# A hybrid attention and RWKV layer on one core: last group of the output projection by tiles, rotary rows double-buffered, small loads moved to the first phase

## Chip, core, metric

One Trainium2 chip, one of its cores. The metric is the device time of one execution in microseconds. TensorE (PE) multiplies matrices, VectorE (DVE), ScalarE (ACT) and GpSimd (POOL) compute element by element, and SyncE (SP) and ScalarE issue transfers (DMA).

## Reference

The layer takes 1024 prompt rows and 64 sample rows of width 1024, normalises them, sends them through one projection, and runs two groups of heads on its columns: differential attention (8 heads) and RWKV-7 (16 heads of 64). Cut to what matters here:

```python
h = _rms_norm(x, norm_pre, NORM_EPS)
proj = h @ w_in
q = _partial_rope(proj[..., A_Q:A_K].reshape(...), pos)      # the first 16 of 64 dims
k = _partial_rope(proj[..., A_K:A_V].reshape(...), pos)
lam = (jnp.exp(jnp.sum(lam_q1 * lam_k1)) - jnp.exp(jnp.sum(lam_q2 * lam_k2)) + lambda_init)
o = _diff_attend(q, k_all, v_all, pos, k_pos, lam)           # sample rows: cached k and v ahead
...
yb, s_T = _wkv_scan(rh, hs(decay), kh, vh, -kk, kk * ah, wkv0)
...
mix = jnp.concatenate([y_a, yb], axis=-1)                    # 2048 wide, both gated
out = mix @ w_out                                            # 2048 x 1024
x_new = x + _rms_norm(out, norm_post, NORM_EPS)
```

## The kernel before

All products are in fp32 precision: both operands are split into a rounded part and the rest (`wh`/`wl`, `hhi`/`hlo`, `mxh`/`mxl`), and three matmuls make one product. ScalarE makes the rounded part (a cast), POOL the rest (a subtraction; the helper's line is L158 for both the mix and the weights).

The work has four parts. The first normalises the rows and projects the first columns. `phase_b` runs the RWKV units, a chain of small steps on DVE, ScalarE and TensorE, while `filler()` projects the remaining columns as work for TensorE in between. `phase_a` runs attention head by head: `prep(h)` loads `qa`, `ka` (each in four transfers, from `rots` and `scr` in DRAM), the cached keys `ck`, and `vl`, `vn`, `ga`, and casts them to `qs` and `k`; scores `s`, exponentials `e`, transposed weights `wt` and outputs `x_o` follow. `out_projection` multiplies the mix with `w_out` and is woven with attention, except for its end.

Of the q and k columns the first 16 dims of each head are rotated. `proj` stores them in DRAM (`rots[kd, g, 0]` and, with the halves swapped, `rots[kd, g, 1]`; kd is q or k, g one of two sets of four heads), and `rope(kd, g)` handles them in 8 chunks of 136 columns: three loads on ScalarE's queue (`ra`, `rb`, `rt`, one buffer each for q and for k), three DVE operations (L965 to L967), and a store on SP's queue. The attention of head 0 needs `(q, 0)` and `(k, 0)`, that of head 4 `(q, 1)` and `(k, 1)`.

`out_projection` has groups (L1054): a range of k tiles of 128 rows and the column halves of 512. A job is a group and one of nine token tiles (the ninth has the 64 sample rows). `load_wo(g)` loads and splits a group's weights in pieces of 256 columns (`wor`, 4 buffers), `load_mix(q)` a job's mix. Groups 0 to 5 have four k and one half; 6 and 7 have two k and both halves. Each half's product comes in a PSUM tile (two of these) and is added to `part` by DVE (L1157). After its last group a tile is finished: sum of squares on ScalarE, two small steps on POOL (L1126, and the power -0.5 in L1127), then columns 0 to 767 on DVE (L1130, L1132) and the other 256 on ScalarE and POOL (L1129, L1131, L1133), where `npb` is the weight of the last norm and `fx` the input rows.

Two things set the order. `Weave` simulates costs and emits streams by rank (`yield` gives a stream's waiting time or condition); then a scheduler makes one list per engine, with tiles and their buffers. Each engine runs its list in order. Transfers go over eight lanes, and a transfer waits for the earlier one on its lane.

Of the kernel before, what the change touches and what calls it, by code (L numbers as in the profile page):

```python
# [1040 lines left out]
def out_projection(tc, I, O, E):  # L1041

    nc = tc.nc
    mm, act, stt, vtt, gtt, gts = (E[k] for k in ("mm", "act", "stt", "vtt", "gtt", "gts"))
# [72 lines left out]

    def finish(tt):
        o_ = part[tt]
        n = P if tt < 8 else TS  # L1120
        x_ = op.tile([P, D], F32, tag="x", bufs=2, name=f"fx{tt}")
        nc.scalar.dma_start(out=x_[:n], in_=x_rows(tt))
        sq = op.tile([P, D], BF16, tag="sq", name=f"fs{tt}")
        ms = op.tile([P, 1], F32, tag="ms", bufs=2, name=f"fm{tt}")
# [361 lines left out]
```

## Time and profile before

| | |
|---|---|
| three timed runs, median (lowest to highest) | 1856.12 us (1855.7 to 1856.61) |
| profiled execution: its own time | 1855.12 us |
| its span in the trace | 1853.3 us |
| busy in the span | PE 1691.8, DVE 1254.4, ACT 849.8, POOL 737.2 us |

The span is 1.8 us shorter than the time of the same execution; the rest lies around it. The windows below are in microseconds from the start of the span: RWKV with filler lies up to about 1246, attention begins after 1258, the output projection alone fills the end from about 1710. Row groups below carry line numbers of the kernel before.

### The profile page before, as it was taken

To read this page: it belongs to the slowest core of one execution; us is meant where nothing else is said; L and a number is where in the kernel's file an instruction comes from. 1 tells how busy PE (TensorE), PEld (TensorE's weight loads), DVE (VectorE), ACT (ScalarE), POOL (GpSimd) and SP (SyncE) were. 2 spreads that over 40 slices of the span, in tenths; PEclk is the share of its full clock that TensorE was granted. 3 is DMA by queue.
4 is the path that set the end of the run, shared out by engine and by line. 5 is a ranking of instruction groups with operands and counts; after the bars stand their busy time and mean duration, and the time that the engine had idled before them with its cause. 6 is when DMAs were issued, how large, how long until landed. Compare 5 with 4: busy or idle time off the path is not lost. (4 is left out here: it accounts for less than half of the span.)

```text
span 1853.3 us, 34474 instructions
## 1 busy us (share of the span) xinstructions
PE 1691.8 (91%) x12930; PEld 1505.7 (81%) x12930; DVE 1254.4 (68%) x2588; ACT 849.8 (46%) x2027; POOL 737.2 (40%) x938
## 2 busy tenths in 40 slices
PE   6999899899998999999999899997889888999995
PEld 5888888888888888888888789886879777787883
DVE  5568777777777787886876776524576655676236
ACT  5534444344344344434343434333556566576323
POOL 4442333233233333323332322113434456666757
PEclk8999999999999999999999899997999889999998
DMA  4110111231122110111101122345555655454425
GB/s 145 50 56 27 50 48 48 79 86 35 39 72 61 52 45 30 39 52 34 57 24 49 51 64 58 88 114 160 158 152 151 179 134 146 126 152 127 121 85 183
DMA packets 204240, 158.82 MB, mean 86 GB/s; under 512 B 44229, under 2 KB 185194, under 8 KB 204074
## 3 DMA queue, kind: packets, MB, share of 16 engines
q1 hardware_dynamic: 169242, 137.33, 25.8%
q10 hardware_dynamic: 34832, 19.30, 4.1%
q8 instruction: 102, 1.67, 0.4%
q14 instruction: 64, 0.52, 0.1%
HBM read 108.67 MB, written 47.34 MB: 84 GB/s over the span
## 5 line engine op out<-in xcount | busy, mean ns | idle before, releaser
L1146 PE MATMUL po<-woh,mxh 128*128 128x512 f32 x288 | 120.9, 420 | 7.4 <-DVE part L1157 5.9
L1147 PE MATMUL po<-woh,mxl 128*128 128x512 f32 x288 | 115.9, 402 | 2.4 <-POOL mxl L158 2.4
L1340 ACT ACTIVATE e<-s,nb 128x128 f32<-128x128 f32 (+7 forms) x144 | 101.0, 706 | 35.2 <-DVE nb L1333 19.7
L1148 PE MATMUL po<-wol,mxh 128*128 128x512 f32 x288 | 115.0, 400 | 1.9 <-POOL wol L158 1.9
L158 POOL TENSOR_TENSOR mxl<-mxr,mxh 128x512 fp32r<-128x512 f32 (+1 forms) x72 | 86.4, 1201 | 75.3 <-ACT mxh L157 66.7
L812 ACT ACTIVATE sd<-suv,dc 64x64 f32<-64x64 f32 x128 | 44.4, 347 | 152.9 <-DVE suv L843 148.7
L1323 PE MATMUL s<-k,qs 128*128 128x512 f32 (+4 forms) x208 | 80.0, 393 | 20.4 <-ACT k L1250 11.4
L1333 DVE TENSOR_REDUCE nb<-s 128x1 f32<-128x640 f32 (+8 forms) x104 | 95.8, 922 | 2.2
L1157 DVE TENSOR_TENSOR part<-po,part 128x512 f32<-128x512 f32 x72 | 49.6, 689 | 69.7 <-PE po L1148 69.6
L1384 PEld LDWEIGHTS x_o<-vn,wt 128*128 128x128 f32 (+1 forms) x608 | 80.1, 199 | 19.9 <-DVE wt L1374 5.8
L1384 PE MATMUL x_o<-vn,wt 128*128 128x128 f32 (+1 forms) x608 | 86.9, 289 | 9.9 <-DVE wt L1374 5.4
L833 PE MATMUL cbank<-suv,bkt 128*128 128x128 f32 x256 | 57.3, 306 | 36.3 <-DVE suv L829 36.1
L843 DVE SCALAR_TENSOR_TENSOR suv<-cbank,dc,sd 64x64 f32<-64x64 f32 x224 | 63.1, 282 | 32.0 <-PE cbank L833 27.9
L833 PEld LDWEIGHTS cbank<-suv,bkt 128*128 128x128 f32 x256 | 41.2, 190 | 50.8 <-DVE suv L829 48.4
L1324 PE MATMUL s<-k,qs 128*128 128x512 f32 (+4 forms) x208 | 73.8, 372 | 3.0 <-POOL k L1253 2.3
L215 PE MATMUL pj_v<-hhi,wh_v 128*128 128x384 f32 (+1 forms) x192 | 70.3, 366 | 6.3 <-DVE mg L416 5.8
L157 ACT CAST mxh<-mxr 128x512 fp32r<-128x512 f32 (+1 forms) x72 | 40.9, 569 | 74.5 <-PE po L1148 32.2
L678 POOL TENSOR_TENSOR ltlo<-lt,lt 64x512 f16<-64x512 f32 x32 | 37.5, 1170 | 93.4 <-ACT lt L666 92.2
L1146 PEld LDWEIGHTS po<-woh,mxh 128*128 128x128 f32 x288 | 55.1, 191 | 21.1 <-DVE part L1157 4.5
L215 PE MATMUL pj_k<-hhi,wh_k 128*128 128x384 f32 (+1 forms) x192 | 67.7, 353 | 4.0 <-ACT raw_k L230 4.0
L215 PE MATMUL pj_aq<-hhi,wh_aq 128*128 128x384 f32 (+1 forms) x192 | 70.0, 365 | 0.5 <-DVE fl_g L940 0.3
L215 PE MATMUL pj_av<-hhi,wh_av 128*128 128x384 f32 (+1 forms) x192 | 69.4, 362 | 0.9 <-DVE fl_g L940 0.9
(531 smaller groups left out, 6115.0 us busy)
## 6 DMA issues: line engine op xcount, KB each, us to landing
mxr<-mixB SPq DMA_DIRECT2D x32, 256.0 KB
wor<-in_w_out SPq DMA_DIRECT2D x64, 128.0 KB
qa<-scr_q SPq DMA_DIRECT2D x32, 204.0 KB
ka<-scr_k SPq DMA_DIRECT2D x32, 204.0 KB
scr_q<-fl_q SPq DMA_DIRECT2D x8, 544.0 KB
scr_k<-fl_k SPq DMA_DIRECT2D x8, 544.0 KB
scr_v<-fl_v SPq DMA_DIRECT2D x8, 544.0 KB
scr_g<-fl_g SPq DMA_DIRECT2D x8, 544.0 KB
```

Source lines behind the costliest of these rows:

```text
L158: gtt(lo, raw, hi.bitcast(F32), op=SUB)
L215: mm(ps[:, :n], hi[:, k, :], hhi[i][:, k, :], start=(k == 0), stop=False)
L833: mm(s, bkt[:, c], suv[:, c], start=True, stop=True)
L843: stt(suv[r, c + 1, h, :] if c < 7 and not smp else to[r], s[r, h * CH:(h + 1) * CH], dc[r, c:c + 1], sd[r], op0=MUL, op1=ADD)
L1146: mm(ps, hi[:, q, :], wh, start=(q == 0), stop=False)
L1147: mm(ps, lo[:, q, :], wh, start=False, stop=False)
L1148: mm(ps, hi[:, q, :], wl, start=False, stop=(q == len(ks) - 1))
L1323: mm(s2[:, b:b + w], lq, k1[c][:, k0 + o_:k0 + o_ + w], start=True, stop=False)
L1324: mm(s2[:, b:b + w], lq, k2[c][:, k0 + o_:k0 + o_ + w], start=False, stop=True)
L1333: nc.vector.tensor_reduce(nb[:, 0:m], s3[:, :, 0:n], axis=AX.X, op=MAX, negate=True)
L1340: act(e[:, 0:n], s3[:, j, 0:n], AF.Exp, bias=nb[:, j:j + 1], accum_out=st["sm"][:, c:c + 1])
L1384: mm(ops[:, 0:P], wt[0:w, b, :], vn[0:w, vb, :], start=(b == 0), stop=(b == len(kbs) - 1))
```

## The change

Four parts:

1. **Output projection.** Groups 6 and 7 become one group 6 (`LAST`) with k 4 to 7 and both halves, so there are 63 jobs in place of 81. Its eight weight tiles take four tags of their own beside the four shared ones; `load_wo(LAST)` starts at job 47 instead of at the start of a group. The sum of squares is made by halves (`half_done`), the two sums and the eps term are added on DVE (L1160), and only the power stays on POOL (L1161). For seven of nine tiles DVE does all 1024 columns (L1166, L1167); tiles 3 and 8 keep the 768/256 split. `npb` is multiplied once by the root of D, since the sum is no longer divided by D.
2. **Ropes.** `ra`, `rb`, `rt` get two buffers each, the loads of chunk j + 1 are issued ahead of the computation of chunk j, and only one rope runs at a time.
3. **Loads.** The four loads of the lambda vectors (`lv`) and the two of the cached keys of head 0 (`ck0`) are issued in the first phase.
4. **Casts.** Of four casts of `xa` and `xw` in the first phase three go to VectorE.

```diff
+    for i, nm in enumerate(("lam_q1", "lam_k1", "lam_q2", "lam_k2")):
+        nc.scalar.dma_start(out=lv[:, i, :], in_=I[nm][0:1, :].to_broadcast([P, 64]))
+    for r in range(2):
+        nc.scalar.dma_start(out=ck0[:, :, r, :], in_=I["cache_k"][0, 0, :, 0])
...
-            nc.scalar.copy(xw[0:64], wa[0:64])
-            nc.scalar.copy(xa[64:128], wa[64:128])
-            for x, r, minus in ((xw, slice(64, 128), gtt), (xa, slice(0, 64), vtt)):
-                nc.scalar.copy(x[r], aw[r])
+            nc.vector.tensor_copy(xa[64:128], wa[64:128])
+            nc.vector.tensor_copy(xw[0:64], wa[0:64])
+            for x, r, copy, minus in ((xw, slice(64, 128), nc.scalar.copy, gtt),
+                                      (xa, slice(0, 64), nc.vector.tensor_copy, vtt)):
+                copy(x[r], aw[r])
...
+                a = rp.tile([P, W], F32, tag="ra", bufs=2, name=f"ra{kd}{g}{j}")
+                b = rp.tile([P, W], F32, tag="rb", bufs=2, name=f"rb{kd}{g}{j}")
+                tb = rp.tile([P, 2, W], F32, tag="rt", bufs=2, name=f"rt{kd}{g}{j}")
...
+            yield lambda: not rope_on
+            rope_on.append(1)
+            ahead = load_rot(0)
+            yield W_LD / 2
+            for j in range(8):
+                cl, a, b, tb = ahead
+                if j < 7:
+                    ahead = load_rot(j + 1)
+                yield W_LD / 2
                 vtt(a, a, tb[:, 0, :], op=MUL)
                 vtt(b, b, tb[:, 1, :], op=MUL)
                 vtt(a, a, b, op=ADD)
...
-              (range(4, 6), (0, 1)), (range(6, 8), (0, 1))]
+              (range(4, 8), (0, 1))]
+    LAST = 6
+    vts(npb, npb, math.sqrt(D), None, op0=MUL)
...
-        for i, (k, ch) in enumerate((k, ch) for k in ks for ch in chs):
-            t = 4 * (g % 2) + i
+        for i, (k, ch) in enumerate((k, ch) for ch in chs for k in ks):
+            t = 4 * (g % 2 if i < 4 else 2) + i % 4
...
-            if q % 9 == 0:
+            if q % 9 == 0 and g < LAST:
                 yield lambda: done[0] >= 9 * (g - 1)
                 weave.add(99.2, load_wo(g))
+            elif q == 9 * LAST - 7:
+                weave.add(99.2, load_wo(LAST))
...
+    def half_done(tt, ch):
+
+        if ch == 0:
+            x_ = op.tile([P, D], F32, tag="x", bufs=2, name=f"fx{tt}")
+            nc.scalar.dma_start(out=x_[:P if tt < 8 else TS], in_=x_rows(tt))
+            fin[tt] = x_, op.tile([P, 2], F32, tag="ms", bufs=2, name=f"fm{tt}")
+        sq = op.tile([P, 512], BF16, tag="sq", name=f"fs{tt}{ch}")
+        act(sq, part[tt][:, ch * 512:(ch + 1) * 512], AF.Square, accum_out=fin[tt][1][:, ch:ch + 1])
...
-        gts(ms, ms, 1.0 / D, NORM_EPS, op0=MUL, op1=ADD)
-        gtt(ms, ms, nh[:, 0:1], op=POW)
-        a, b = o_[:, 0:768], o_[:, 768:]
-        act(b, b, AF.Copy, scale=ms)
-        stt(a, a, ms, npb[:, 0:768], op0=MUL, op1=MUL)
-        gtt(b, b, npb[:, 768:], op=MUL)
-        vtt(a[:n], a[:n], x_[:n, 0:768], op=ADD)
-        gtt(b[:n], b[:n], x_[:n, 768:], op=ADD)
+        vts(ms[:, 0:1], ms[:, 0:1], ms[:, 1:2], D * NORM_EPS, op0=ADD, op1=ADD)
+        gtt(ms[:, 0:1], ms[:, 0:1], nh[:, 0:1], op=POW)
+        m = 768 if tt in (3, 8) else D
+        a, b = o_[:, 0:m], o_[:, m:]
+        if m < D:
+            act(b, b, AF.Copy, scale=ms[:, 0:1])
+        stt(a, a, ms[:, 0:1], npb[:, 0:m], op0=MUL, op1=MUL)
+        vtt(a[:n], a[:n], x_[:n, 0:m], op=ADD)
+        if m < D:
+            gtt(b, b, npb[:, m:], op=MUL)
+            gtt(b[:n], b[:n], x_[:n, m:], op=ADD)
...
-    for i, nm in enumerate(("lam_q1", "lam_k1", "lam_q2", "lam_k2")):
-        nc.scalar.dma_start(out=lv[:, i, :], in_=I[nm][0:1, :].to_broadcast([P, 64]))
```

How the lists of the engines move is shown at three places. In the rows, `x<-a,b` is a tile written from tiles read, the number behind a name is the tile's own, and the size of the output follows.

POOL's list ahead of group 5, before. Here the names keep their numbers: `wol31` is the rest of the weight of k tile 3, second half, in two pieces from `wor310` and `wor31256`; `mxl45` is the rest of the mix of group 4, token tile 5:

```order
L158 TENSOR_TENSOR wol31_21317<-wor310_21318,woh31_21316 128x256
L158 TENSOR_TENSOR mxl43_21142<-mxr43_21119,mxh43_21141 128x512
L158 TENSOR_TENSOR wol31_21317<-wor31256_21322,woh31_21316 128x256
L158 TENSOR_TENSOR mxl44_21162<-mxr44_21135,mxh44_21161 128x512
L158 TENSOR_TENSOR mxl45_21182<-mxr45_21155,mxh45_21181 128x512
L158 TENSOR_TENSOR mxl46_21202<-mxr46_21175,mxh46_21201 128x512
L1099 MEMSET mxr48_21215 128x512
L158 TENSOR_TENSOR mxl47_21223<-mxr47_21195,mxh47_21222 128x512
L158 TENSOR_TENSOR mxl48_21247<-mxr48_21215,mxh48_21246 128x512
L158 TENSOR_TENSOR mxl50_21269<-mxr50_21240,mxh50_21268 128x512
L158 TENSOR_TENSOR mxl51_21295<-mxr51_21262,mxh51_21294 128x512
```

The list from its later part on after the change; `wol40` and `wol50` are of the last group:

```order
L158 TENSOR_TENSOR mxl47_21224<-mxr47_21196,mxh47_21223 128x512
L158 TENSOR_TENSOR mxl48_21248<-mxr48_21216,mxh48_21247 128x512
L158 TENSOR_TENSOR mxl50_21270<-mxr50_21241,mxh50_21269 128x512
L158 TENSOR_TENSOR mxl51_21300<-mxr51_21263,mxh51_21299 128x512
L158 TENSOR_TENSOR wol40_21278<-wor400_21279,woh40_21277 128x256
L158 TENSOR_TENSOR wol40_21278<-wor40256_21319,woh40_21277 128x256
L158 TENSOR_TENSOR wol50_21328<-wor500_21329,woh50_21327 128x256
L158 TENSOR_TENSOR wol50_21328<-wor50256_21339,woh50_21327 128x256
L158 TENSOR_TENSOR mxl52_21316<-mxr52_21291,mxh52_21315 128x512
L158 TENSOR_TENSOR wol31_21334<-wor31256_21343,woh31_21333 128x256
```

The second piece of `wol31`, which group 5 needs in its first job, stood next but one behind the first; now it is behind `mxl50`, `mxl51`, four pieces of the last group's weights, and `mxl52`.

ScalarE's list at the transition to attention, before; the DMA rows are issues on its queue:

```order
L943 ACTIVATE fl_v_15361<-pj_av_0_15362 128x384
L1182 DMA lv<-in_lam_q 128x64
L1182 DMA lv<-in_lam_k 128x64
L1182 DMA lv<-in_lam_q 128x64
L1182 DMA lv<-in_lam_k 128x64
L1222 DMA ck_15299<-in_cache_k 128x2x64 x2
L1227 DMA vn_15314<-in_cache_v 128x128
L943 ACTIVATE fl_v_15361<-pj_av_1_15400 128x384
L1227 DMA vn_15856<-in_cache_v 128x128
```

The same place after the change (`ck_15897` is that of head 1):

```order
L952 ACTIVATE fl_v_15401<-pj_av_0_15402 128x384
L1265 DMA vn_15358<-in_cache_v 128x128
L1260 DMA ck_15897<-in_cache_k 128x2x64 x2
L952 ACTIVATE fl_v_15401<-pj_av_1_15434 128x384
L1265 DMA vn_15912<-in_cache_v 128x128
L952 ACTIVATE fl_v_15401<-pj_av_2_15466 128x320
```

The lambda loads and the first `ck` are gone from here; they are the first six issues of ScalarE's list now, ahead of `bd`, which stood first.

DVE's list after the transition, before (`raq`, `rbq` are a chunk of q1, `rak`, `rbk` one of k1, `wt_2` a copy that TensorE needs for `x_o`):

```order
L965 TENSOR_TENSOR raq_15390<-raq_15390,rtq_15392 128x136
L967 TENSOR_TENSOR raq_15390<-raq_15390,rbq_15391 128x136
L940 SCALAR_TENSOR_TENSOR fl_g_15467<-fl_g_15467,pj_ag_1_15499 128x384
L966 TENSOR_TENSOR rbk_15507<-rbk_15507,rtk_15508 128x136
L965 TENSOR_TENSOR rak_15506<-rak_15506,rtk_15508 128x136
L940 SCALAR_TENSOR_TENSOR fl_g_15467<-fl_g_15467,pj_ag_2_15546 128x320
L967 TENSOR_TENSOR rak_15506<-rak_15506,rbk_15507 128x136
L966 TENSOR_TENSOR rbq_15534<-rbq_15534,rtq_15535 128x136
L965 TENSOR_TENSOR raq_15533<-raq_15533,rtq_15535 128x136
L967 TENSOR_TENSOR raq_15533<-raq_15533,rbq_15534 128x136
L966 TENSOR_TENSOR rbk_15708<-rbk_15708,rtk_15709 128x136
L1374 COPY wt_2_15828<-x_wt_20_15879 128x384
```

The rows ahead of the same copy after the change:

```order
L986 TENSOR_TENSOR rbk_15617<-rbk_15617,rtk_15618 128x136
L986 TENSOR_TENSOR rbk_15682<-rbk_15682,rtk_15683 128x136
L949 SCALAR_TENSOR_TENSOR fl_g_15513<-fl_g_15513,pj_ag_2_15586 128x320
L985 TENSOR_TENSOR rak_15616<-rak_15616,rtk_15618 128x136
L987 TENSOR_TENSOR rak_15616<-rak_15616,rbk_15617 128x136
L985 TENSOR_TENSOR rak_15681<-rak_15681,rtk_15683 128x136
L987 TENSOR_TENSOR rak_15681<-rak_15681,rbk_15682 128x136
L986 TENSOR_TENSOR rbk_15782<-rbk_15782,rtk_15783 128x136
L986 TENSOR_TENSOR rbk_15931<-rbk_15931,rtk_15932 128x136
L985 TENSOR_TENSOR rak_15781<-rak_15781,rtk_15783 128x136
L987 TENSOR_TENSOR rak_15781<-rak_15781,rbk_15782 128x136
L1412 COPY wt_2_15884<-x_wt_20_15939 128x384
```

Chunks of q1 and k1 alternated; now only chunks of k1 stand here, in pairs, and seven of the eight are ahead of `wt_2`. The rest of q1 stands in the last RWKV unit.

## Rows read from the trace of the kernel before

**Rows 1.** Windows: busy us (x instructions) of each engine, clock, DMA share, GB/s.
```profile
1180.00:1200.00 20.00, 15.78 (x102) 14.38 (x102) 13.29 (x35) 4.72 (x11) 5.04 (x5) 1.00 0.47 126
1270.00:1400.00 130.00, 116.13 (x733) 104.77 (x733) 77.47 (x164) 65.87 (x172) 55.52 (x75) 0.98 0.57 153
1760.00:1805.00 45.00, 45.00 (x200) 37.28 (x199) 17.29 (x25) 11.95 (x28) 24.89 (x31) 1.00 0.29 87
1810.00:1845.00 35.00, 23.81 (x88) 15.95 (x86) 26.63 (x32) 14.35 (x29) 29.95 (x39) 0.95 0.63 216
```

**Rows 2.** Forms of 1811 to 1853 us: busy, mean ns, idle before and releasers.
```profile
L1146 PE MATMUL po<-woh,mxh 128*128 128x512 f32 x27 | 11.7, 434 | 7.1 <-DVE part L1157 5.9 <-ACT mxh L157 1.1
...
L1130 DVE SCALAR_TENSOR_TENSOR part<-part,fm,npb 128x768 f32<-128x768 f32 x9 | 10.8, 1199 | 7.5 <-POOL fm L1127 7.5
L1133 POOL TENSOR_TENSOR part<-part,fx 128x256 f32<-128x256 f32 x8 | 10.4, 1296 | 0.5
L1157 DVE TENSOR_TENSOR part<-po,part 128x512 f32<-128x512 f32 x15 | 10.2, 683 | 1.5 <-PE po L1148 1.5
L1131 POOL TENSOR_TENSOR part<-part,npb 128x256 f32<-128x256 f32 x9 | 9.8, 1085 | 3.7 <-ACT part L1129 3.7
...
L1132 DVE TENSOR_TENSOR part<-part,fx 128x768 f32<-128x768 f32 x8 | 8.4, 1051 | 0.1
...
L158 POOL TENSOR_TENSOR mxl<-mxr,mxh 128x256 fp32r<-128x256 f32 x5 | 4.5, 892 | 0.0
L1127 POOL TENSOR_TENSOR fm<-fm,nh 128x1 f32<-128x1 f32 x8 | 4.4, 549 | 0.7
L1126 POOL TENSOR_SCALAR fm<-fm 128x1 f32<-128x1 f32 x8 | 2.1, 265 | 0.7
```

**Rows 3.** Timeline, TensorE, first score matmul: start us, us, instruction [idle before].
```profile
1258.67 0.80 PE L1323 MATMUL s<-k,qs 128*128 128x128 f32 x2 [10.58 <-ACT k L1250]
```

**Rows 4.** Waits of SP's DMA queue, 1237 to 1262 us: total us, times, longest.
```profile
SPq L1208 <- DMA ck<-in_cache_k: 3.6, 2, 2.3
SPq L1208 <- DMA lv<-in_lam_q: 3.3, 1, 3.3
SPq L1207 <- DMA ck<-in_cache_k: 2.8, 1, 2.8
SPq L1207 <- DMA lv<-in_lam_q: 2.1, 1, 2.1
```

**Rows 5.** Forms on POOL, 1733 to 1800 us, output projection.
```profile
L158 POOL TENSOR_TENSOR mxl<-mxr,mxh 128x512 fp32r<-128x512 f32 x16 | 20.6, 1292 | 11.2 <-ACT mxh L157 11.1
L158 POOL TENSOR_TENSOR wol<-wor,woh 128x256 fp32r<-128x256 f32 x22 | 15.7, 738 | 0.3 <-ACT woh L157 0.3
```

**Rows 6.** Timeline near the end.
```profile
1837.33 1.47 DVE L1130 SCALAR_TENSOR_TENSOR part<-part,fm,npb 128x768 f32<-128x768 f32 x1 [0.92 <-POOL fm L1127]
...
1841.32 0.63 PE L1148 MATMUL po<-wol,mxh 128*128 128x512 f32 x1
...
1845.97 1.02 DVE L1130 SCALAR_TENSOR_TENSOR part<-part,fm,npb 128x768 f32<-128x768 f32 x1 [0.72 <-POOL fm L1127]
```

**Rows 7.** DMA view, 1237 to 1262 us: totals.
```profile
DMA packets 3087, 3.89 MB, mean 156 GB/s; under 512 B 2017, under 2 KB 2323, under 8 KB 3085
```

**Rows 8.** Timeline of DVE, 1284 to 1306 us, rope steps and `wt_2`.
```profile
1284.43 0.30 DVE L966 TENSOR_TENSOR rbq<-rbq,rtq 128x136 f32<-128x136 f32 x1 [4.77 <-DMA rtq<-in_c_rot]
...
1298.38 0.30 DVE L966 TENSOR_TENSOR rbq<-rbq,rtq 128x136 f32<-128x136 f32 x1 [4.08 <-DMA rbq<-rot_q]
...
1305.34 0.30 DVE L966 TENSOR_TENSOR rbk<-rbk,rtk 128x136 f32<-128x136 f32 x1 [4.11 <-DMA rbk<-rot_k]
1305.56 0.55 DVE L1374 COPY wt<-x_wt 128x384 f32<-128x384 f32 x1
```

**Rows 9.** Waits of DVE, 1170 to 1240 us.
```profile
DVE raq L965 <- DMA raq<-rot_q: 5.2, 1, 5.2
```

**Rows 10.** Waits of TensorE, 50 to 64 us.
```profile
PE pj_k L215 <- ACT raw_k L230: 4.0, 1, 4.0
```

More of the change, by code (lines that the diff above doesn't have):

```diff
@@ L270, in layer @@
     vts(hsl, pc(R_SL), 0.5 * (1.0 - LAMBDA_INIT), None, op0=MUL)
+    lv = cst.tile([P, 4, 64], F32, name="lv")
+    for i, nm in enumerate(("lam_q1", "lam_k1", "lam_q2", "lam_k2")):
+        nc.scalar.dma_start(out=lv[:, i, :], in_=I[nm][0:1, :].to_broadcast([P, 64]))
+    ls = cst.tile([P, 2], F32, name="ls")
+    nlam = cst.tile([P, 1], F32, name="nlam")
+    ck0 = cst.tile([P, 2, 2, 64], F32, name="ck0")
+    for r in range(2):
+        nc.scalar.dma_start(out=ck0[:, :, r, :], in_=I["cache_k"][0, 0, :, 0])
     mixed = set()
@@ L955, in rope, with load_rot @@
             W = T // 8
-            for j in range(8):
+            def load_rot(j):
                 cl = slice(j * W, (j + 1) * W)
-                a = rp.tile([P, W], F32, tag="ra", name=f"ra{kd}{g}{j}")
-                b = rp.tile([P, W], F32, tag="rb", name=f"rb{kd}{g}{j}")
-                tb = rp.tile([P, 2, W], F32, tag="rt", name=f"rt{kd}{g}{j}")
+                a = rp.tile([P, W], F32, tag="ra", bufs=2, name=f"ra{kd}{g}{j}")
+                b = rp.tile([P, W], F32, tag="rb", bufs=2, name=f"rb{kd}{g}{j}")
+                tb = rp.tile([P, 2, W], F32, tag="rt", bufs=2, name=f"rt{kd}{g}{j}")
                 nc.scalar.dma_start(out=a, in_=E["rots"][kd, g, 0][:, cl])
@@ L1061, in there @@
         return (None, 2) in mixed if j == 2 else all((p, j) in mixed for p in range(8))
-    jobs = [(g, tt) for g in range(8) for tt in ((4, 5, 6, 7, 0, 1, 2, 3, 8) if g == 7 else range(9))]
+    jobs = [(g, tt) for g in range(7) for tt in ((4, 5, 6, 7, 0, 1, 2, 3, 8) if g == LAST else range(9))]
     ws = {}
@@ L1120, in finish @@
         n = P if tt < 8 else TS
[L1121 to L1124, printed above, removed]
-        act(sq, o_, AF.Square, accum_out=ms)
-        gts(ms, ms, 1.0 / D, NORM_EPS, op0=MUL, op1=ADD)
-        gtt(ms, ms, nh[:, 0:1], op=POW)
-        a, b = o_[:, 0:768], o_[:, 768:]
-        act(b, b, AF.Copy, scale=ms)
-        stt(a, a, ms, npb[:, 0:768], op0=MUL, op1=MUL)
-        gtt(b, b, npb[:, 768:], op=MUL)
-        vtt(a[:n], a[:n], x_[:n, 0:768], op=ADD)
-        gtt(b[:n], b[:n], x_[:n, 768:], op=ADD)
+        x_, ms = fin.pop(tt)
+        vts(ms[:, 0:1], ms[:, 0:1], ms[:, 1:2], D * NORM_EPS, op0=ADD, op1=ADD)
[9 more added lines that the diff above has]
+            gtt(b[:n], b[:n], x_[:n, m:], op=ADD)
         dst = O["xp"][0, tt * P:(tt + 1) * P, :] if tt < 8 else O["xs"][0]
@@ L1177, in phase_a @@
     psx = E["ctx"].enter_context(tc.tile_pool(name="psx", bufs=2, space=PSUM, reuse_waits="tile"))
-    lv = ap_.tile([P, 4, 64], F32, name="lv")
-    for i, nm in enumerate(("lam_q1", "lam_k1", "lam_q2", "lam_k2")):
-        nc.scalar.dma_start(out=lv[:, i, :], in_=I[nm][0:1, :].to_broadcast([P, 64]))
+    lv, ls, nlam, ck0 = (E[k] for k in ("lv", "ls", "nlam", "ck0"))
     vtt(lv[:, 0::2, :], lv[:, 0::2, :], lv[:, 1::2, :], op=MUL)
-    ls = ap_.tile([P, 2], F32, name="ls")
     nc.vector.tensor_reduce(ls, lv[:, 0::2, :], axis=AX.X, op=ADD)
     act(ls, ls, AF.Exp)
-    nlam = ap_.tile([P, 1], F32, name="nlam")
     vtt(nlam, ls[:, 1:2], ls[:, 0:1], op=SUB)
@@ L1219, in prep @@
             nc.gpsimd.memset(q[:, T:QW], 0.0)
-        ck = ap_.tile([P, 2, 2, 64], F32, tag="ck", name=f"ck{h}")
-        for r in range(2):
-            nc.scalar.dma_start(out=ck[:, :, r, :], in_=I["cache_k"][0, 0, :, h])
+        if h == 0:
+            ck = ck0
+        else:
+            ck = ap_.tile([P, 2, 2, 64], F32, tag="ck", name=f"ck{h}")
+            for r in range(2):
+                nc.scalar.dma_start(out=ck[:, :, r, :], in_=I["cache_k"][0, 0, :, h])
         ks_ = [load_dup("k", h, c) for c in range(2)]
```

12 lines of the change are left out of this document (8 added, 4 removed).

## Prediction

> **What bounds the kernel now.** I read the busy time of the engines by stretch first. In 1760–1805 us TensorE is busy 45.00 of 45.00 us with 200 matmuls, one every 0.225 us: there the time is its own work, and nothing that this change does can shorten it. In 1810–1845 it is busy 23.81 of 35.00 us with 88 matmuls, while POOL is busy 29.95; in 1270–1400 it is idle 13.9 of 130.00; in 1180–1200 it is idle 4.2 of 20.00 [rows 1]. A gain can only come from the places where TensorE waits, and I read each of them for what it waits for.
>
> At the end, the forms of 1811–1853 show TensorE's idle time, 7.1 us, put down mostly to `part` additions on DVE; DVE itself idles 7.5 us before the scaling at L1130, for `fm` from POOL [rows 2]. Following it back, POOL has for every tile `mxl` 0.89, the two `fm` steps 0.27 and 0.55, `npb` 1.09 and `fx` 1.30: 4.1 us on its busiest tiles against 12 matmuls (2.7 us) per tile of group 7. POOL sets the pace of the last nine tiles.
>
> Between the RWKV part and attention, TensorE waits 10.6 us, to 1258.67, for `k` from ScalarE [rows 3]; `k` is cast from `ka`, whose loads SP issues. SP's queue stood for earlier transfers of `lv` and `ck`: 3.6 + 3.3 + 2.8 + 2.1 = 11.8 us [rows 4], because a transfer waits for the earlier one on its lane.
>
> **The output projection.** Groups 6 and 7 become one with both halves and four k. Matmuls stay the same in number; the mix is split 9 times (512 wide) in place of 18 times (256 wide); POOL keeps `mxl` and the power alone, 1.29 + 0.55 = 1.84 us per tile of 24 matmuls (5.40 us) [rows 2, 5]. So POOL stops pacing. The 88 matmuls at 0.225 us take 19.8 us from 1810, where the last one now ends at 1841.32 + 0.63 = 1841.95 [rows 6]: a gain of 12.1 at most; counting only its idle time up to there (31.95 − 23.81) gives 8.1. I take 10.5, nearer to the count, since matmuls that follow each other closely show 0.225.
>
> DVE takes over. Per tile: two additions 2 × 0.68, the scaling of 1024 columns in place of 768, 1.20 × 4/3 = 1.60, the residual 1.05 × 4/3 = 1.40, and one small step, put at 0.27 like POOL's own, plus 0.55 of waiting for the power [rows 2]: 5.2 us against 5.40. That just fits; hand-offs between engines of some 0.1 us each may push it over, and only two PSUM tiles stand between it and TensorE. Bounds 0 to +5, taken +1. After the last matmul the chain keeps its length: a Square of half the width gives back about what the second `part` addition of tile 8 loses by standing behind the two 768-column steps of tile 3. I put 0, ±1.5.
>
> In group 5, POOL must now split the weights of half more tiles before the last group: 16 × 0.74 + 9 × 1.29 = 23.4 us [rows 5] beside 108 matmuls, 24.3 us. POOL's list shows the second half of `wol31`, which group 5's first job needs, behind `wol40` and `wol50` of the last group, and these write buffers that group 4 uses to its end. From there POOL has four pieces, `mxl52` and the half itself, 5 × 0.74 + 1.29 = 5.0 us, some 5.5 with ScalarE's first cast; the first job needs it after 9 of its 12 matmuls, 2.0 us. TensorE stands 3.5 us; less, if other jobs' data bring the pieces earlier. Bounds 0 to +5, taken +3.
>
> The scaling of `npb`, once 1024 columns, falls into DVE's idle time at the start of the projection: 0, or its 1.4 us at most.
>
> Here a rule of the Trainium skill speaks against the change. The trace first: the scaling of 768 columns takes 1.47 us beside POOL's work where the group's shortest is 1.02 (last tile, POOL idle at its start) [rows 6], so 0.45 us is lost, not POOL's whole instruction. The Trainium skill, "SBUF — State Buffer", section "Who interferes with whom", says that a DVE instruction with two SBUF inputs and a reading GpSimd instruction exclude each other for their whole duration. By it every `mxl` would hold DVE up in full, and the last group would come out as in the second rival below; by the trace a part of it.
>
> **Lambda and the first cached keys.** The six loads go to the head of ScalarE's queue in the first phase; SP's list of `qa`, `ka`, `vl`, `ga` keeps its order. The lanes then hold only `qa`/`ka` themselves. Gain at most the 11.8 us that SP stood [rows 4], and little more than the 10.6 of TensorE's wait [rows 3]. It will not all come: with the queue free, the bytes still have to move. `qa` and `ka` are eight transfers each of 68 and 204 KB, 2.2 MB of the 3.89 MB that moved in 25 us at 156 GB/s [rows 7]; at that rate they take 14 us from 1238, to 1252, and landing, cast and the first matmul another 3 (an estimate): TensorE goes on at 1255 in place of 1258.7, a gain of 3.7. At 216 GB/s, which 1810–1845 shows [rows 1], they take 10 us, and the gain is 7.6. I take −7, since less else is under way ahead of them; bounds −3 to −12.
>
> **The ropes.** Chunks are 16 sets of three small DVE operations; only when they run matters. q0 and k0 lie far ahead of their use, beside RWKV work that keeps TensorE supplied with projection matmuls: 0; without that cover they would cost what q1's do. The chunks of q1 and k1 alternated after 1270, one step per 7.0 us ((1305.34 − 1284.43)/3), each step a DMA wait with DVE standing [rows 8]. Now all of q1 lies before the transition, and k1 comes in pairs. In 1270–1400 TensorE's 13.9 idle us [rows 1] bound what can come back; part of them lies behind `wt` copies that stand behind rope steps on DVE. The order puts seven of k1's eight chunks ahead of the copy `wt_2`, which ran at 1305.56 directly behind the fourth waiting step [rows 8]. If a pair takes what one and a quarter steps take now (8.5 us), three pairs, from the first chunk's end at about 1277 (a step ahead of 1284.43), end at 1277 + 25.5 = 1302.5, no later than now, and the waits after 1310 are gone. Taken −4, a third of the 13.9; bounds −10 to +6. The four further chunks of q1 come into the last RWKV unit, whose DVE work is a chain: the first chunk there cost DVE 5.2 us [rows 9], TensorE's idle time around was 4.2 us. Four more at 0 to 2 us each: taken +2, bounds 0 to +8.
>
> **The start.** At 54–60 us TensorE waits 4.0 us for `raw_k`, a ScalarE copy behind the casts of `xa` and `xw` [rows 10]; one cast of 1.1 us less stands after the late arrival of `aw`, so −1.1; the three that DVE takes (some 1.2 us each, like ScalarE's) fall where DVE waits for `wa` and `aw`, and would give that gain back if DVE had other work. The six new loads stand ahead of the first activation and can make it later by their issue and lane waits: 0 to +2, taken +0.6. Sum −0.5; bounds −1.5 to +2.
>
> **The sum.** −10.5 + 1 + 3 − 7 − 4 + 2 − 0.5 = −16. The profiled execution took 1855.12 us; 1839.1 follows, and the median of the timed runs is 1.0 above it (1856.12): **1840**. Faster or slower means by over 0.2%, 3.7 us, about what can be told from no change.
>
> **Rivals.**
> *Bytes, not queues (chance 0.20).* The transfers of the transition are as many as before but for lambda (4 × 32 KB) and two `ck` (2 × 64 KB); if the engines of the DMA were full all the while, only 0.26 MB/156 GB/s = 1.6 us comes back there, and the ropes, bound by round trips, give 0 on balance. Then −10.5 + 4 − 1.6 − 0.5 = −8.6: 1847.5. For it: 3.89 MB in that stretch [rows 7]; against: SP stood 11.8 us for transfers of 32 and 64 KB. The Trainium skill, "DMA: Bandwidth & Descriptors", section "Issuing engines are not separate DMA queues", says that all transfers end on the same 16 engines whichever engine issues them; by that rule this rival is right, and SP's waits are only where the shortage shows.
> *DVE paces the last group (0.10).* If each `mxl` (1.29) adds in full to DVE's 5.2 per tile, it needs 6.5 against 5.40: nine tiles give +9.9 in place of +1, so 1849.
> *All of it comes (0.12).* Tail −12, 3 lost in group 5, transition −11, ropes −6, start −1: −27, 1829.
> *The ropes hold the chain (0.07 slower, 0.06 no change).* With two buffers a chunk's load still waits for the store of the chunk two before. In the old trace the same stream's next chunk came 13.95 us later (1284.43 to 1298.38) [rows 8]. If a pair takes that, three pairs ahead of `wt_2` end at 1277 + 42 = 1319, 13 us later than now, and TensorE, which keeps its order, stands for all of it; at 5.2 us for each of q1's four further chunks 21 more come in the RWKV chain. Against −14 from the other parts (−16 without the −4 and +2) it decides from 14 us on, which takes the first in full and some of the second; with both in full, 34 − 14 = +20: 1876. No change lies at a hold-up of 10 to 18 us. That double-buffering overlaps nothing is part of this rival.
>
> **How the numbers follow.** The forecast has 0.45, its own range 1834 to 1846; 0.20 and 0.10 lie at 1847–1849, 0.12 near 1829, 0.13 above 1852. A range from 1829 to 1852 leaves out the last, and half of the case "all of it". Faster 0.87, same 0.06, slower 0.07.
>
> **What would show it.** Tail: TensorE dense to about 1812 + the shift and its wait for `part` at most 2 us in all; POOL below half busy; DVE the busiest but TensorE in the last 40 us. Group 5: one wait of TensorE for `woh31` or `wol31` in its first job, some 3 us, and none after it. Transition: the wait of `s` for `k` at 3 to 6 us in place of 10.6, and no wait of SP for `lv` or `ck` there. Ropes: DVE's waits for `rb` and `ra` in 1270–1400 gone after the first 35 us, and `wt_2` no later than now against the transition's end. The prediction is wrong if DVE paces the tail, if SP's waits merely change their name to `qa` and `ka` at the same length, or if TensorE shows more than 6 us of idle time in 1180–1240.

## The result, and the profile of the changed kernel

The changed kernel takes 1840.37 us (median of 4 runs, 1838.66 to 1845.82) against 1856.25 us before (4 runs, 1855.7 to 1856.61). The ratio is 0.9926, 95% interval 0.9912 to 0.9941: 15.9 us less by the medians, 13.7 by the ratio. The forecast was 1840, range 1829 to 1852.

Its first profiled execution was the longest of the four, 1845.82 us with a span of 1844.0. A second one, taken with the last experiments (run `changed_again`), had 1836.08 and 1834.3. Both are read here, since the difference between them turns out to be part of the story.

Two windows of the changed kernel, first execution; the first begins as far behind the first matmul of attention as that of [rows 1], the second is the end. Columns are those of [rows 1]:

```profile
1275.80:1405.80 130.00, 123.80 (x790) 113.24 (x790) 82.36 (x167) 71.17 (x186) 58.34 (x77) 0.98 0.57 153
1798.00:1833.00 35.00, 34.15 (x150) 27.62 (x148) 25.18 (x32) 12.19 (x31) 10.04 (x12) 1.00 0.59 193
```

The end window of [rows 1] reaches 3 us past the last matmul. The 35 us up to the last matmul of the kernel before are:

```profile
1807.00:1842.00 35.00, 26.81 (x101) 18.44 (x99) 25.32 (x32) 14.51 (x30) 28.19 (x37) 0.96 0.58 202
```

So in the 35 us up to its last matmul TensorE now has 150 matmuls in place of 101, and POOL is busy 10.04 us in place of 28.19. In the stretch of the ropes its idle time is 6.2 us in place of 13.9.

The forms of the end, 1793 to 1844 us, same execution, beside [rows 2]:

```profile
L1183 PE MATMUL po<-woh,mxh 128*128 128x512 f32 x57 | 22.4, 392 | 0.9 <-DVE part L1194 0.9
...
L1194 DVE TENSOR_TENSOR part<-po,part 128x512 f32<-128x512 f32 x15 | 10.3, 684 | 4.6 <-PE po L1185 4.6
...
L1166 DVE SCALAR_TENSOR_TENSOR part<-part,fm,npb 128x1024 f32<-128x1024 f32 x6 | 9.7, 1624 | 4.2 <-POOL fm L1161 4.2
L1167 DVE TENSOR_TENSOR part<-part,fx 128x1024 f32<-128x1024 f32 x7 | 8.5, 1218 | 0.1
```

TensorE now waits 0.9 us for `part` in place of 5.9, and DVE waits for TensorE (4.6 us) instead of holding it up.

The longest wait of TensorE from 1710 us to the end, same execution:

```profile
PE po L1183 <- ACT woh L157: 1.4, 1, 1.4
```

It is that of group 5's first job; beside it there are the 0.9 us for `part` and 0.2 us for `wol`. The transition, TensorE's timeline (beside [rows 3]), same execution:

```profile
1264.45 0.80 PE L1361 MATMUL s<-k,qs 128*128 128x128 f32 x2 [6.66 <-ACT k L1288]
```

And the waits of SP's queue there, 1243 to 1265 us, those on which `qa` or `ka` stood for small loads of ScalarE's queue (beside [rows 4]):

```profile
SPq L1242 <- DMA vn<-in_cache_v: 2.9, 2, 2.6
...
SPq L1243 <- DMA ck<-in_cache_k: 0.5, 1, 0.5
```

The 11.8 us for `lv` and `ck` have become 3.4 for `vn` and the `ck` of head 1. The rope steps of k1 and `wt_2`, timeline of DVE (beside [rows 8]):

```profile
1285.79 0.30 DVE L986 TENSOR_TENSOR rbk<-rbk,rtk 128x136 f32<-128x136 f32 x1 [2.00 <-DMA rbk<-rot_k]
...
1297.49 0.62 DVE L986 TENSOR_TENSOR rbk<-rbk,rtk 128x136 f32<-128x136 f32 x1 [3.44 <-DMA qa<-rot_q]
...
1304.26 0.30 DVE L986 TENSOR_TENSOR rbk<-rbk,rtk 128x136 f32<-128x136 f32 x1 [3.36 <-DMA rbk<-rot_k]
...
1309.42 0.55 DVE L1412 COPY wt<-x_wt 128x384 f32<-128x384 f32 x1
```

Three pairs begin 11.7 and 6.8 us apart, and `wt_2` comes 45.0 us behind the first matmul of attention; before it was 46.9 (1305.56 − 1258.67).

To see where time went over the whole program, take the same matmul in two traces: TensorE's list has 12930 in each, in nearly the same order. The table gives the n-th matmul's start before, and by how many us it is later (+) or earlier in other profiled executions (four of them are explained below):

```
   n   before   changed  changed  output   loads   ropes   first
                1st      2nd      alone    alone   alone   ropes single
 100     33.6    +2.5     +1.5     -0.3    +2.6    +0.6     +1.5
 150     48.2    +2.6     -2.7     -0.3    +2.6    -0.8     +1.5
2300    310.9    +2.9     -1.7     -0.3    +2.7    +0.8     +1.5
2800    376.5    +4.8     -1.3     -0.2    +2.4    +1.0     +1.1
4200    542.1    +5.0     -1.1     -0.1    +2.5    +1.4     +1.1
4650    597.8    +8.2     +0.2     -2.1    +2.1    +4.2     -0.4
9400   1164.4    +8.7     -0.7     -3.4    +1.8    +4.0     -0.7
9850   1233.2   +11.2     +0.6     -2.0    +1.6    +4.7     +0.4
10000  1278.7    +4.5     -7.5     -1.1    -3.6    +3.5     -6.7
10600  1387.0    -2.6    -14.8     +1.7    -1.3    -3.3    -14.5
12600  1754.8    -1.5    -13.6     +3.1    -0.8    -2.8    -13.1
12650  1766.1    +2.2     -7.5     +7.4    -0.8    -2.8    -11.1
12850  1811.4    +3.6     -6.1     +8.8    -0.8    -2.8     -9.1
12929  1841.3    -8.3    -18.1     -3.2    -0.8    -3.9    -21.0
```

Read a part of the change from the step between two lines: 2300 to 2800 has the ropes of q0, 4200 to 4650 those of k0, 9400 to 9850 those of q1; 9850 to 10000 is the transition, 10000 to 10600 the ropes of k1, 12600 to 12650 the start of group 5, 12650 to 12850 the rest of it and the first half of the last group (which begins at 12714), 12850 to the end the last tiles. A step in one execution is not yet an effect: where other kernels are named below, their steps were read from their profiled executions in the same way.

### The profile page after: what moved, and what is told of

It is laid out like the page before. It is cut to its first block, busy times and chain, and to the rows that moved or that the text cites. A ratio compares the mean times of both kernels' runs of the same rounds, so it can differ in the third digit from the quotient of the medians.

```text
span 1844.0 us, 34363 instructions
## 1 busy us (share of the span) xinstructions
PE 1697.7 (92%) x12930; PEld 1516.1 (82%) x12930; DVE 1254.7 (68%) x2583; ACT 846.3 (46%) x2026; POOL 720.6 (39%) x905
## 5 line engine op out<-in xcount | busy, mean ns | idle before, releaser
L158 POOL TENSOR_TENSOR mxl<-mxr,mxh 128x512 fp32r<-128x512 f32 x63 | 84.5, 1344 | 66.1 <-ACT mxh L157 56.5
L1361 PE MATMUL s<-k,qs 128*128 128x512 f32 (+4 forms) x208 | 77.9, 383 | 13.5 <-ACT k L1288 7.4
L1194 DVE TENSOR_TENSOR part<-po,part 128x512 f32<-128x512 f32 x54 | 37.2, 689 | 67.2 <-PE po L1185 67.1
L1362 PE MATMUL s<-k,qs 128*128 128x512 f32 (+4 forms) x208 | 72.0, 363 | 3.4 <-POOL k L1291 2.7
L215 PE MATMUL pj_r<-hhi,wh_r 128*128 128x384 f32 (+1 forms) x192 | 71.0, 370 | 0.0
L215 PE MATMUL pj_ak<-hhi,wh_ak 128*128 128x384 f32 (+1 forms) x192 | 70.2, 366 | 0.0
```

Of the source, the lines that this page charges most:

```text
L158: gtt(lo, raw, hi.bitcast(F32), op=SUB)
L215: mm(ps[:, :n], hi[:, k, :], hhi[i][:, k, :], start=(k == 0), stop=False)
L1361: mm(s2[:, b:b + w], lq, k1[c][:, k0 + o_:k0 + o_ + w], start=True, stop=False)
L1362: mm(s2[:, b:b + w], lq, k2[c][:, k0 + o_:k0 + o_ + w], start=False, stop=True)
```

## Experiments

Ratios are to the kernel before on the same chip, with 95% intervals; a ratio of 0.001 is 1.9 us. There are 12 runs of each of the first four kernels and 4 to 6 of each of the others. The first four put one part of the change on the kernel before.

**Output projection alone** (part 1 of the diff).

```diff
-              (range(4, 6), (0, 1)), (range(6, 8), (0, 1))]
+              (range(4, 8), (0, 1))]
...
```

> Only the output projection's part of the change, on the kernel before. Theory (the terms read from the two traces): the last matmul ends 12 us earlier against the matmuls at 1811, and 3 to 4 us of this are lost at the first job of group 5, where TensorE waits for woh31 and wol31: -8 us, 1848. Rival: the loss at group 5 comes from the changed order of the other parts and is absent here: -12 us, 1844. Second rival: DVE paces the last group by itself: -4 us or less.

Measured: 1847.07 us, ratio 0.9956 (0.9944 to 0.9969), −8.2 us. The theory's value. The table shows both halves of it: +4.3 us at group 5's start, +1.4 in the first half of the last group, and −12.0 behind 1811. The loss at group 5 belongs to this part by itself.

**Loads alone** (part 3).

```diff
+    for i, nm in enumerate(("lam_q1", "lam_k1", "lam_q2", "lam_k2")):
+        nc.scalar.dma_start(out=lv[:, i, :], in_=I[nm][0:1, :].to_broadcast([P, 64]))
...
```

> Only the lambda and first cached-key loads moved to the first phase. Theory: the wait of the first score matmul for k falls from 10.6 to about 6.7 us as in the changed kernel, some 6 us come back in the transition, and the six issues at the head of ScalarE's list make the first rows 2.5 us later: -4 us, 1852. Rival (bytes): SP's waits only change their name, -2 in the transition, +2.5 at the start: no change.

Measured: 1853.58 us, ratio 0.9984 (0.9967 to 1.0001), about −3, which is not quite clear of no change. TensorE's wait for `k` is 7.18 us, and the table has +2.6 at the start and −5.2 in the transition, as the theory said. The +2.3 in the rope stretch behind it (10000 to 10600) can't be put down to the loads: the run with the output projection alone, which leaves loads and ropes as they were, has +2.8 there, and in both the granted clock of the stretch is 0.95 where it was 0.98.

**Ropes alone** (part 2).

```diff
-                a = rp.tile([P, W], F32, tag="ra", name=f"ra{kd}{g}{j}")
+                a = rp.tile([P, W], F32, tag="ra", bufs=2, name=f"ra{kd}{g}{j}")
...
```

> Only the double-buffered ropes. Theory: q0 (320 to 380 us) and k0 (535 to 610) now hold DVE ahead of the RWKV chain and cost 2.3 and 3.4 us, q1 costs 3, and 1280 to 1400 gives 7 back: +1.7, 1858, no change that can be told. Rival: the losses at q0 and k0 come with the other parts' new places on the lanes, and the ropes alone give -4 us, 1852.

Measured: 1851.52 us, ratio 0.998 (0.9966 to 0.9995), −3.7. The time is the rival's, but not its reason: k0 does cost 2.8 us here (4200 to 4650), without the other parts; q0 and q1 cost only 0.2 and 0.7, and 10000 to 10600 gives 6.8.

**Casts alone** (part 4).

```diff
-            nc.scalar.copy(xw[0:64], wa[0:64])
-            nc.scalar.copy(xa[64:128], wa[64:128])
+            nc.vector.tensor_copy(xa[64:128], wa[64:128])
+            nc.vector.tensor_copy(xw[0:64], wa[0:64])
...
```

> Only the three casts on VectorE. Theory: raw_k's copies on ScalarE come 1.1 us earlier, TensorE's wait of 4.0 us at 56 us shrinks by that: -1.1 us, 1855. Rival: a wait follows that takes it back (DVE late for the RWKV chain): 0.

Measured: 1855.67 us, ratio 1.0006 (0.9994 to 1.0018): no difference. TensorE's wait for `raw_k` is 3.9 us where it was 4.0 [rows 10]. ScalarE's timeline shows why:

```profile
52.48 1.11 ACT L384 ACTIVATE wa<-wa 64x1088 f32<-64x1088 f32 x1 [2.67 <-DVE wa L370]
57.67 1.09 ACT L393 CAST xw<-aw 64x1088 fp32r<-64x1088 f32 x1 [4.08 <-DMA aw<-wa]
```

The Tanh (L384) ends at 53.59, and the one cast left on ScalarE waits 4.08 us for `aw`, a transfer that begins there. The casts taken off ScalarE had lain in that wait: the one that is left needs the second half of `aw`, which SP issues 1 us behind the first (53.62 after 52.66).

The four ratios add up to −8.2 − 3.0 − 3.7 + 1.1 = −13.8 us; the whole change has −13.7. But each ratio is known to some 2 to 3 us only, and run again the whole change has −18.0 (below), so an interplay of the parts of up to 5 us can't be excluded.

The next three are each meant to mend one loss of the changed kernel. **Weights of the last group one job later.**

```diff
-            elif q == 9 * LAST - 7:
+            elif q == 9 * LAST - 6:
```

> The changed kernel with the weights of the last group started one job later (job 48), which puts the second piece of wol31 back next but one behind its first on POOL. Theory: the 3.8 us that TensorE loses between 1757 and 1764 us are that piece's place and vanish; some 1.4 us at the start of the last group stay: -3.8 us against the changed kernel, 1837. Rival: POOL and ScalarE have too much to split in group 5 anyway (16 pieces and 9 mixes in 24 us), the loss moves to the start of the last group: 0.

Measured: 1836.85 us, ratio 0.9891 (0.9872 to 0.991). The changed kernel, run with the last experiments, has 0.9903, so −2.2 us with overlapping intervals: the time alone does not tell. Window around the start of group 5, changed kernel (second execution), then the mended one:

```profile
1747.00:1758.00 11.00, 10.33 (x33) 8.10 (x34) 2.08 (x3) 5.76 (x14) 9.93 (x13) 0.69 0.56 173
```

```profile
1746.00:1757.00 11.00, 11.00 (x51) 9.09 (x50) 2.77 (x4) 5.39 (x14) 11.00 (x14) 1.00 0.62 187
```

33 matmuls against 51. The wait is 2.92 us (its row stands below), and the window holds only the last 0.7 us of it. The clock is 0.69 over the window: behind the wait 13 matmuls come 0.43 us apart in place of 0.227, at the lower of TensorE's two levels (1.2 in place of 2.4 GHz), and that costs about as much again as the wait. In the mended kernel there is no wait for `woh` and no fall, but POOL is busy all 11.00 us of its window, and five jobs later, still in group 5, TensorE waits for a piece of the mix:

```profile
1762.64 0.50 PE L1184 MATMUL po<-woh,mxl 128*128 128x512 f32 x1 [0.98 <-POOL mxl L158]
```

Up to the last group's first matmul (12600 to 12714) this kernel loses 1.6 us, and the three kernels below that have this edit too lose 2.7, 2.9 and 3.1, with waits for `mxl` of 1.7 to 2.2 us. With the weights at job 47 the loss there is 1.9 to 6.1 us in six executions, 3.5 in the mean. So the edit gives about 1 us in the mean. The rival named the reason, POOL's share in group 5; the loss moves, though not as far as the start of the last group.

**The loads behind the casts.** Two small copies on POOL write into `lv` and `ck0` first, so that the six loads can't go ahead.

```diff
+            nc.gpsimd.tensor_copy(lv[:, :, 0], wa[:, 0:4])
+            nc.gpsimd.tensor_copy(ck0[:, :, :, 0], wa[:, 0:4].rearrange("p (c r) -> p c r", r=2))
+            for i, nm in enumerate(("lam_q1", "lam_k1", "lam_q2", "lam_k2")):
+                nc.scalar.dma_start(out=lv[:, i, :], in_=I[nm][0:1, :].to_broadcast([P, 64]))
...
```

> The changed kernel with the lambda and first cached-key loads issued behind the casts of xa and xw at about 60 us (two small copies on POOL write the tiles first and hold them back). Theory: the first rows come as early as before, TensorE's sequence is 2.5 us earlier by 40 us and stays so, and the transition's gain is kept: -2.5 us, 1838. Rival: the 2.5 us are lost to the next wait in the RWKV chain or to the later places of transfers on the lanes: 0.

Measured: 1834.63 us, ratio 0.9886 (0.9868 to 0.9904), about −3 against 0.9903. The 100th matmul starts at 33.9 us, where it was 33.6 before the change and 36.1 and 35.0 in the changed kernel. The theory held for the place; the size is inside the noise of the ratio. The start also varies by itself: the eight executions without the six loads ahead lie 0.3 us before to 1.4 behind the 33.6, the six with them 1.5 to 2.6 behind. The means are 1.4 us apart.

**The ropes of the first four heads as before** (a buffer of their own, no load ahead).

```diff
+            n, o = (2, "") if g else (1, "0")
...
-                a = rp.tile([P, W], F32, tag="ra", bufs=2, name=f"ra{kd}{g}{j}")
+                a = rp.tile([P, W], F32, tag=f"ra{o}", bufs=n, name=f"ra{kd}{g}{j}")
...
```

> The changed kernel with the ropes of the first four heads as before (one buffer, no load ahead), those of the second four double-buffered. Theory: TensorE's delays in 320 to 380 us (2 us) and 535 to 610 us (3 us) come from their denser DVE and ScalarE steps and vanish: -4 us, 1836. Rival: these delays are only reshuffled against waits of the RWKV chain: 0.

Measured: 1833.96 us, ratio 0.988 (0.9862 to 0.9898), −4.3 against 0.9903, the theory's value, though the intervals overlap a little. In the changed kernel (second execution) TensorE's waits in 535 to 562 us begin with

```profile
PE m_iq L704 <- DVE q L698: 2.4, 2, 1.8
```

and that wait is gone in this run. It shows in each of the six executions with double-buffered first ropes (1.9 to 3.7 us between 530 and 605) and in none of the eight with single ones. In its table column q0 costs −0.4 and k0 −1.5 where the first execution of the changed kernel had +1.9 and +3.2, the second +0.4 and +1.3. Over the same six and eight executions k0's step is +0.4 to +3.2 against −2.2 to 0; the means of q0 and k0 together are 4.2 us apart, so the traces show this loss and the time agrees.

**All tiles split between the engines**, in the changed kernel.

```diff
-        m = 768 if tt in (3, 8) else D
+        m = 768
```

> The changed kernel with the last columns of all nine tiles (256 of 1024) on ScalarE and POOL, as before the change, instead of two tiles only. Theory: what the old end lacked was POOL time per tile (4.1 us against 2.7 of matmuls); with one mix of 512 per tile POOL needs 1.29 + 0.55 + 1.09 + 1.30 = 4.2 against 5.4, so the merged group alone gives the gain and this is the same time within 1 us. Rival: DVE and POOL get in each other's way and POOL's power comes late behind its other work, so that the part additions wait again: +4 us.

Measured: 1838.22 us, ratio 0.9904 (0.9886 to 0.9922) against 0.9903: the theory, as far as times can tell. It was enough to give POOL 24 matmuls per tile instead of 12. The traces show a small gain of DVE's share all the same. With all tiles split TensorE waits longer for `part`, 2.3 us from 1700 us to the end in place of 0.9:

```profile
PE po L1183 <- DVE part L1194: 2.3, 4, 1.0
```

and the matmuls of the last group take 2.0 us longer; after the last one 9.5 us pass in place of 10.6, so about 1 us is left. The rival's waits were there at a quarter of its price.

The last four ran on one chip together. **The changed kernel again**:

> The changed kernel once more, on the same chip as the mended ones. Theory: its profiled execution of 1845.8 us was a long one; the same kernel varies by several us, since places where TensorE has gaps run at half clock for a longer or shorter stretch. Median 1840 to 1842, the profiled execution may lie anywhere from 1836 to 1846, and the differences against the first profile sit at the gaps (340, 580, 1040, 1200, 1270, 1760 us). Rival: the first profile is typical and the others are faster by chance: median 1845.

Measured: 1838.21 us (1834.36 to 1840.27), ratio 0.9903 (0.9885 to 0.9921), a little below what the theory gave; the profiled one took 1836.08. The table's two columns of the changed kernel part at the gaps that were named, and, with 4.3 of the 9.8 us at the end, at one that was not (36 to 50 us, last section). The wait of group 5's first job in this execution, 1700 us to the end:

```profile
PE po L1183 <- ACT woh L157: 2.9, 1, 2.9
```

The wait for `part` is 0.9 us again.

**All three mends:**

> Weights of the last group one job later, the six loads behind the casts, and the first four heads' ropes single, together. Theory: the three losses are in different places and add up: 3.8 + 2.5 + 4 below the changed kernel, 1830. Rival: they share the same slack in the RWKV chain, and the sum is that of the best alone: 1834.

Measured: 1830.79 us (1829.9 to 1832.52), ratio 0.9866 (0.985 to 0.9881). That is −6.9 against the changed kernel, between the theory's −10.3 and the rival's −4; the three single mends by their ratios (−2.2, −3.2, −4.3) had −9.7. One reason to expect less than the theory is that the loss in group 5 is moved and not removed, 2.7 us here. It beats both kernels: on that chip the one before has a median of 1854.88, 24.1 us more.

**The mends with all tiles split:**

> The three mends, and the last 256 columns of all nine tiles on ScalarE and POOL. Theory: same time as the three mends within 1 us, or 1 to 2 us more for POOL's late power. Rival: DVE paces the last group at 5.2 us per tile and half of that is given back: -3 us.

Measured: 1831.64 us, ratio 0.9873 (0.9855 to 0.9892): the same within the noise. The traces repeat the small difference: the last group's matmuls take 2.2 us longer than with the mends alone, the end after them 1.1 us less. DVE doesn't pace the last group.

**The mends with `ga` held back:**

```diff
+        if h == 0:
+            nc.gpsimd.tensor_copy(ga[:, 0:1], ks_[1][:, 0:1])
         nc.sync.dma_start(out=ga, in_=scr["g", h])
```

> The three mends, and the load of ga of head 0 (0.54 MB, used late) held back until the last ka has landed. Theory (bytes from there on): after the change the transfers fill the engines of the DMA from the first qa to ga, so TensorE's wait for k, 6.7 us in the changed kernel, falls by up to 2 us: -1.5 us. Rival (round trips and lane waits of qa and ka): the wait stays, 0.

Measured: 1830.32 us, ratio 0.9862 (0.9844 to 0.9879) against 0.9866: no difference in time. TensorE's wait for `k` is shorter in the profiled execution, 5.97 us against 7.22 with the mends alone. But the changed kernel with `ga` in its place has 5.87 in one execution, so these 1.25 us lie inside the spread of that wait, and a share of the bytes isn't shown.

## Why the prediction was right, and which terms were off

The forecast and the result agree, and the sum does so in part by errors of both signs. By its terms, with what the two executions of the changed kernel and the single parts showed:

- **The last tiles, −10.5 + 1.** The mechanism held: POOL had set the pace. From the last group's first matmul to its last the gain is 10.6 us in each of the eight executions with this part as it is, where the sum had 9.5: −12.0 behind 12850, next to the count's upper bound of 12.1, since the matmuls come every 0.227 us to the end, and +1.4 ahead of it, where TensorE waits 0.9 us for `part`. After the last matmul 10.6 us pass (1832.98 + 0.39 to 1844.0) where it was 11.3: the 0, ±1.5 held. The reading behind DVE's term did not hold, and that the term came out near is luck. The scaling was taken as 4/3 of a mean of 1.20 us; the mean by the forms above is 1.62, but both means mix two lengths. Timeline, first execution:

```profile
1802.79 1.29 POOL L158 TENSOR_TENSOR mxl<-mxr,mxh 128x512 fp32r<-128x512 f32 x1
1802.86 2.30 DVE L1166 SCALAR_TENSOR_TENSOR part<-part,fm,npb 128x1024 f32<-128x1024 f32 x1 [0.73 <-POOL fm L1161]
...
1805.90 0.47 PE L1183 MATMUL po<-woh,mxh 128*128 128x512 f32 x1 [0.70 <-DVE part L1194]
...
1810.41 1.29 DVE L1166 SCALAR_TENSOR_TENSOR part<-part,fm,npb 128x1024 f32<-128x1024 f32 x1 [0.67 <-POOL fm L1161]
```

  Right behind an `mxl` of 1.29 us the scaling takes 2.30 us, by itself 1.29: of the 1.22 us that the two share, 1.0 is lost. It was the same in the kernel before. The 1.47 us of [rows 6] begin 0.07 us behind this step, and the "POOL's whole instruction" with which the prediction compared the loss of 0.45 us is 0.72 us long:

```profile
1837.26 0.72 POOL L158 TENSOR_TENSOR mxl<-mxr,mxh 128x256 fp32r<-128x256 f32 x1
```

  So a tile needs 2 × 0.68 + 1.29 + 1.22 + 0.21 + 0.55 = 4.6 us of the 5.4, and 5.6 where an `mxl` comes first. That is so in two tiles (scalings at 1796.43 and 1802.86), and TensorE's two waits for `part` follow these. The rule of the Trainium skill ("SBUF — State Buffer", section "Who interferes with whom"), by which the later of two such instructions is blocked until the first ends, agrees with these rows nearly in full, and not only in part as the prediction had it. What failed in the second rival is that each `mxl` would add to DVE's time: most of them meet no scaling. In two (1812.35 and 1817.84) it was POOL that took longer, 1.76 and 1.71 us in place of 1.29.
- **Group 5, +3.** Place and reason were right: the second half of `wol31` stood behind four pieces of the last group's weights. The size is right in the mean and hides a wide spread: 12600 to 12714 has +3.7 and +6.1 in the two executions, +4.2 by itself, and 1.9 to 2.6 in three further kernels with the weights at job 47. The wait for `woh` is 0.9 to 2.9 us. What the term lacked is the clock: in the three executions with waits of 0.9 to 1.1 us no matmul is slower behind them; with 1.4, 2.4 and 2.9 us 8, 6 and 13 matmuls run at the lower level. The Trainium skill, "TensorE: Matmul & The Clock Gate", section "What's actually happening", says that the chip halves TensorE's clock when it has been idle; the 13 matmuls at 0.43 us behind an idle 2.9 us agree. That one edit would take the loss away is not borne out: one job later a wait for `mxl` takes the place of that for `woh`.
- **The transition, −7.** 6.7 and 8.1 us in the two executions, 5.2 by itself. The wait of `s` for `k` is 6.66 and 5.87 us in place of 10.58, where 3 to 6 was named. TensorE's wait of 1.3 us for `ck` itself, which no term had, is gone too. SP's waits for `lv` and the first `ck` are gone; 3.4 us for `vn` and the second `ck` took part of their place. The rival "bytes, not queues" is refuted in its price, 1.6 us. The rule behind it, that all transfers end on the same engines (the Trainium skill, "DMA: Bandwidth & Descriptors", section "Issuing engines are not separate DMA queues"), isn't: no run here tells whether bytes have a share in the wait that is left, since holding back 0.54 MB changed neither the time nor that wait beyond its spread.
- **The ropes of k1, −4.** 7.1 and 7.3 us came back (6.8 alone), nearly twice the term. The sum reasoned from a third of the idle time; the idle time fell from 13.9 to 6.2, and no chunk of q1 stands in the stretch. The section on the kernel before is wrong in one point: `ra`, `rb`, `rt` are one buffer for q and k together, not one for each. So the 7.0 us per step were the whole round trip of a single buffer, and the pairs of two buffers, 11.7 and 6.8 us apart, make it 4.6 per chunk. The price of the last rival (13.95 us per pair) rested on that error.
- **q1 in the last RWKV unit, +2.** 2.5 and 1.3 us (0.7 alone), but the runs of the other three parts, with the ropes as before, have −0.2 to +1.5 there, so no cost of q1 can be told. TensorE is idle 4.4 us in 1180 to 1240, as before. DVE's wait for the first chunk is 5.2 us as before [rows 9], the others wait 1.3 in all.
- **q0 and k0, 0.** This term was wrong. They cost 5.1 us in the first execution, 1.7 in the second, 4.2 in the mean of all executions with and without them, and undoing them gives 4.3. The cover that the prediction named, projection matmuls beside the RWKV chain, didn't hide them: TensorE waits for the chain's `q` on DVE (2.4 us) with the double-buffered ropes, and not without. Why `q` is late wasn't isolated: in DVE's timeline a rope step that waits 1.1 us for its load (541.81, second execution) stands ahead of it, but with steps of the chain in between.
- **The start, −0.5.** The casts' −1.1 did not come: the second half of `aw` arrives after the other casts were done. By the 100th matmul TensorE is 2.5 and 1.5 us late; over all executions the six loads cost 1.4 us, inside the 0 to 2, where 0.6 was taken.

So terms that were too small as gains (1 to 2 us at the end, 3.2 at the ropes of k1) and as losses (some 4 at the first ropes, 2 at the start with the casts, up to 3 in group 5) nearly cancel. That the forecast met the median within half a microsecond is luck; run again, the median is 1838.21. What stays open is how the 15.9 us of the medians divide exactly, since the runs of the changed kernel differ by up to 11 us among themselves. Whether the split between queue and bytes in the transition could be taken further (the load of `vn` moved too) was not tried.

## What to carry to other kernels

When a group at the end is paced by a helper engine, look at work per matmul: merging two small groups gave POOL twice the matmuls per tile and brought 10.6 us, while sharing the columns otherwise brought about 1. Look for where the next stage's pieces stand in a helper's list ahead of the present stage's own, and whether the helper has room for them at all: one job earlier cost 1.9 to 6.1 us here, one job later still 1.6 to 3.1, because POOL was full. Take the length of a step from single instructions, with and without a neighbour beside it, before scaling it: a mean of 1.62 us stood for 1.29 and 2.30. And a prefetch that is put ahead of a chain's steps on a busy engine must be priced there, even if its own result is needed much later.

## What the hardware showed unexpectedly

Two executions of the same program differ by where TensorE's clock is halved. The window 36 to 50 us of the changed kernel, first and second execution:

```profile
36.00:50.00 14.00, 11.88 (x48) 9.61 (x48) 8.84 (x22) 4.67 (x11) 7.52 (x14) 0.63 0.20 54
```

```profile
36.00:50.00 14.00, 12.55 (x75) 11.24 (x76) 10.00 (x23) 7.21 (x16) 9.24 (x18) 1.00 0.20 55
```

The same stretch has 48 matmuls at a granted clock of 0.63 and 75 at 1.00, and the two columns of the table part by 4.3 us from n = 100 to 150. 1.00 is TensorE's level of 2.4 GHz; 0.63 is a stretch that ran in good part at the lower one, 1.2 GHz. In both executions TensorE had just waited for `x` from DVE, 2.12 us in the first (to 38.56) and 2.06 in the second (to 37.43): nearly the same wait, once with a slow stretch behind it and once without. What differs is the 5 us from 31 to 36, with a granted clock of 0.87 in the first and 1.00 in the second. That such stretches make the changed kernel's runs spread from 1834 to 1846 us is likely and not shown; of its nine executions the longest has the lowest mean granted clock, 0.969, and the shortest one of the highest, 0.974. In group 5, too, a gap that is closed can give back more than its own length: the slow stretch behind it, where there is one.
